# One trunk step on one core: p turned ahead by VectorE and kept in memory, the embedding weight in four transfers, and another order at the end

## The chip, the cores and the metric

The kernel runs on one core of a Trainium2 chip. Time is device time of one execution, in microseconds (us). The engines of a core are TensorE (PE in the profile; PEld is its loading of weights), VectorE (DVE), ScalarE (ACT), GpSimd (POOL) and SyncE (SP), each with its own queue of instructions in an order fixed when the program is built. Transfers are issued by SP, POOL or ACT, wait in that engine's queue like any other instruction, and run on 16 shared DMA engines.

## The reference

One layer over 2048 prompt rows and 32 sample rows of width 1024. All is float32.

```
hn   = rmsnorm(h, g_mix)
proj = hn @ w_in                      # 1024 -> 3072: hA bA cA zA vB zB
y    = concat(conv mixer, pooling mixer)
h    = h + y @ w_out                  # 1024 -> 1024
gate = sigmoid(rmsnorm(h, g_ple) @ w_ple_gate)
h    = h + (p @ w_ple) * gate         # p: 256 wide, w_ple: 256 -> 1024
return rmsnorm(h, g_final), states of the two mixers
```

The part that the change is about is `p @ w_ple`, called the embedding here, and the gate's last rows.

## The kernel before

Rows are taken in 17 tiles: 16 of 128 prompt rows and one of 32 sample rows. A float32 product is made of three: each operand is cut into a high and a low part (`split`, L76: ScalarE copies the high part, L77, VectorE subtracts it from the operand, L80), and hi x hi, hi x lo and lo x hi are added up in PSUM. The large products also use seven sub-products in the place of eight (`seven`, L212): two tiles of rows and the halves of the inner and outer dimension make 2 x 2 blocks, sums of blocks are formed by VectorE, and the results are put together from the banks x, y and z.

The stages, in the order of time:

- the input projection in three groups of columns of the turned rows (L580): groups 0 and 1 by seven products, group 2 plainly. Beside a group's products, work for later ones (turning of x, sums of its blocks) is fed in small steps: `at_pace(steps, num, den)` (L1163) takes `num` steps in `den` calls, one call being made at a fixed place in the product. In group 1 this work is `last_block` (L1149), which makes ready the rows of group 2 and stores them by POOL to memory (`b_d`).
- the early embedding: tiles 0 to 2 (`early_embedding`, L1116), begun beside the last products of group 2
- the output product with `w_out` (banks x_o, y_o, z_o, L169), beside which the gate weight is scaled (tiles `gs`, loaded by POOL, stored to `g_d`)
- the rest of the embedding: tiles 3 to 14 and the sample tile as `rest_e`, thirteen in all; the last two of them are run after the first rows for the gate have been turned
- the gate product (x_g, y_g, z_g), pair by pair; with each pair the addition to h, the final norm and the store
- the last pair, tiles 14 and 15 (`last_pair`), with the embedding of tile 15 (bank `e_l`) in it.

`embed` (L106) does the embedding of a list of tiles. `prep` loads four tiles' p at a time by SP (L123, tile `ep`), turns a tile of 128 x 256 by two transposes on TensorE into a PSUM bank (L132, tile `ptp`), and splits it from there into `pps`. `run` keeps two tiles ahead of itself, multiplies (L104, twice six products of 128 x 128 with 512 columns) and ScalarE and SP take the result to memory (`e_d`, L149 and L150). The embedding's weight `w_ple` has two tiles of 128 rows, each loaded by one transfer, at three places (`wp`, `wq`, `wl`).

The gate weight is read back from `g_d` into buffers `xh` (three of them) as `wg_r`, eight loads by SP, and split and summed by VectorE and ScalarE. The rows for the gate are turned on TensorE (`turned`, tile `pth`, L1399) for the upper tile of a pair and the sample tile, and by VectorE (`turned_here`, L1410) for the lower one: a stream transpose turns every 32 x 32 block of a tile, and the load puts the blocks at their places. All these loads are issued by SP.

In the last pair (`finish`, L1488 to L1509; `out`, L1518) each half of a tile runs through the sigmoid (ScalarE), multiplication with the embedding and addition to h (VectorE), a square summed over the row (ScalarE, `junk`), and a multiplication with the final norm's weight (`hg`). When both halves are there, POOL makes the row's factor (L1500 to L1503), VectorE and ScalarE scale half a row each, and the two halves are stored. `between` (argument 5 of `seven`) puts the embedding of tile 15's second half into the middle of the last products; its first half comes after the last.

A planner with estimates of costs sets the order of instructions on each engine, from the program's order, buffers and the estimates; an instruction given to `tc.keep_in_program_order` stays in the program's order.

## Time and profile before

| | |
|---|---|
| median of 3 executions | 929.99 us (929.95 to 930.98) |
| the profiled execution, its own time | 931.64 us |
| its span, first to last instruction | 929.9 us |
| TensorE busy | 914.6 us, 4581 products |
| VectorE, ScalarE, POOL busy | 717.1, 483.4, 127.5 us |
| bytes moved | 190.05 MB, mean 204 GB/s |

Times in the profile are microseconds from the start of the span; "L104" is line 104 of the kernel. In a row of the timeline or the chain the first number is the start, the second the duration. "x12" is a count of instructions taken together. The chain of waits is followed back from the last instruction: at each step to what released it, or to the instruction before it on its engine. A row "engine tile L <- releaser" in the list of waits has total us, times and the longest.

### The profile page before, as it was taken

How to read it: one execution, taken by the hardware profiler on the slowest of the kernel's cores; microseconds unless marked ns; L12 is line 12 of the kernel's file. 1: busy time of each engine (PE TensorE's matmuls, PEld its weight loads, DVE VectorE, ACT ScalarE, POOL GpSimd, SP SyncE). 2: the span in 40 equal slices, each digit the busy share in tenths (PEclk: the TensorE clock that was granted, in tenths of full speed). 3: DMA queues.
4: the chain of work that ended last, by engine and by line, in shares of the span. 5: the costliest groups of instructions: out<-in, count | busy, mean ns of one | idle time of the engine just before them, and what ended most of it. 6: DMA issues, size and time to landing. Idle time of an engine off the chain costs nothing.

```text
span 929.9 us, 13092 instructions
## 1 busy us (share of the span) xinstructions
PE 914.6 (98%) x4581; PEld 827.7 (89%) x4581; DVE 717.1 (77%) x1215; ACT 483.4 (52%) x895; POOL 127.5 (14%) x244
## 2 busy tenths in 40 slices
PE   7999999999999999999999999999999999999996
PEld 6999999999999999999999987888878868888885
DVE  6996989999577778585777679656564797888985
ACT  7744565654445544443545356344344865555664
POOL 3111222121001110000000011112111001111113
PEclk9999999999999999999999999999999999999999
DMA  8357687798935457337665359876775883666563
GB/s 245 100 148 217 173 255 223 222 306 298 408 100 179 136 175 215 96 102 263 200 178 168 127 207 286 241 201 202 222 219 187 309 263 119 215 223 239 184 209 114
DMA packets 133791, 190.05 MB, mean 204 GB/s; under 512 B 11740, under 2 KB 101084, under 8 KB 132445
## 3 DMA queue, kind: packets, MB, share of 16 engines
q1 hardware_dynamic: 117741, 138.78, 47.7%
q0 software_dynamic: 13248, 44.93, 14.9%
q10 hardware_dynamic: 2736, 5.51, 1.9%
q8 instruction: 36, 0.59, 0.3%
q14 instruction: 30, 0.25, 0.1%
HBM read 129.59 MB, written 59.58 MB: 203 GB/s over the span
## 4 chain that ended last, share of the span: by engine, by line
PE 89%; DVE 4%; DMA 3%; ACT 2%; issue 1%; POOL 0%; SPq 0%; POOLq 0%; ACTq 0%; DVEq 0%
PE x_o L169 9%; PE x_g L169 9%; PE x_ch L580 6%; PE x_zab L580 6%; PE x_zbv L580 6%; PE z_g L169 5%; PE z_o L169 4%; PE e L104 4%; PE z_ch L580 3%; PE z_zab L580 3%; PE h L580 3%; PE z_zbv L580 3%; PE b L580 3%; PE za L580 3%; PE zb L580 2%; PE c L580 2%
## 5 line engine op out<-in xcount | busy, mean ns | idle before, releaser
L77 ACT CAST y_S<-y_fS 128x512 fp32r<-128x512 f32 x32 | 19.5, 622 | 42.7 <-PE x_o L169 20.4
L104 PE MATMUL e<-wq,pps 128*128 128x512 f32 (+1 forms) x156 | 38.9, 400 | 0.2 <-ACT pps L77 0.2
L169 PE MATMUL x_g<-wg_b,g_S 128*128 128x512 f32 x128 | 35.9, 390 | 0.0
L169 PE MATMUL x_o<-wo_b,y_S 128*128 128x512 f32 x128 | 35.6, 390 | 0.0
L580 PE MATMUL x_zbv<-B,w_zbv_S 128*128 128x416 f32 x168 | 34.3, 352 | 0.0
L580 PE MATMUL z_ch<-B,w_ch_S 128*128 128x416 f32 x168 | 34.2, 352 | 0.0
L580 PE MATMUL z_zbv<-B,w_zbv_S 128*128 128x416 f32 x168 | 34.1, 351 | 0.0
L580 PE MATMUL z_zab<-B,w_zab_S 128*128 128x416 f32 x168 | 34.1, 351 | 0.0
L580 PE MATMUL x_zab<-B,w_zab_S 128*128 128x416 f32 x168 | 34.1, 351 | 0.0
L580 PE MATMUL x_ch<-B,w_ch_S 128*128 128x416 f32 x168 | 34.0, 351 | 0.0
L104 PEld LDWEIGHTS e<-wq,pps 128*128 128x128 f32 (+1 forms) x156 | 27.4, 182 | 7.0 <-ACT pps L77 0.5
L580 PEld LDWEIGHTS x_ch<-B,w_ch_S 128*128 128x128 f32 x168 | 31.4, 188 | 0.3
L580 PEld LDWEIGHTS z_zbv<-B,w_zbv_S 128*128 128x128 f32 x168 | 31.3, 188 | 0.3
L580 PEld LDWEIGHTS x_zab<-B,w_zab_S 128*128 128x128 f32 x168 | 31.4, 188 | 0.3
L580 PEld LDWEIGHTS z_zab<-B,w_zab_S 128*128 128x128 f32 x168 | 31.3, 188 | 0.3
L580 PEld LDWEIGHTS z_ch<-B,w_ch_S 128*128 128x128 f32 x168 | 31.3, 188 | 0.4
L580 PEld LDWEIGHTS x_zbv<-B,w_zbv_S 128*128 128x128 f32 x168 | 31.2, 188 | 0.4
L69 POOL TENSOR_SCALAR ms_f<-ssq_f 128x1 f32<-128x1 f32 (+1 forms) x15 | 8.8, 586 | 161.4 <-ACT junk L90 161.4
L77 ACT CAST y<-y 128x512 fp32r<-128x512 f32 x24 | 14.9, 619 | 28.7 <-PE x_o L169 14.1
L1237 DVE TENSOR_TENSOR c_o<-x_o,x 128x512 f32<-128x512 f32 x14 | 9.7, 692 | 25.3 <-PE x_o L169 25.3
L414 DVE SCALAR_TENSOR_TENSOR xt<-xt,rstd_x,g_bc 128x1024 f32<-128x1024 f32 (+2 forms) x14 | 17.9, 1282 | 14.5 <-POOL rstd_x L73 13.4
L1438 DVE SCALAR_TENSOR_TENSOR h<-h,rstd_f,g_bc 128x1024 f32<-128x1024 f32 (+1 forms) x15 | 19.3, 1285 | 12.7 <-POOL rstd_f L73 12.7
(583 smaller groups left out, 2677.6 us busy)
## 6 DMA issues: line engine op xcount, KB each, us to landing
y<-y_d SPq DMA_DIRECT2D x16, 512.0 KB, 9.5
x<-in_x_prompt_dram SPq DMA_DIRECT2D x16, 512.0 KB, 6.0
h_d<-x SPq DMA_DIRECT2D x16, 512.0 KB, 4.2
h<-h_d SPq DMA_DIRECT2D x16, 512.0 KB, 3.9
xt<-in_x_prompt_dram SPq DMA_DIRECT2D x15, 512.0 KB, 7.1
e<-e_d SPq DMA_DIRECT2D x15, 512.0 KB, 5.3
out_dram<-h POOLq DMA_DIRECT2D x14, 512.0 KB, 3.0
p_dT<-T POOLq DMA_DIRECT2D x12, 512.0 KB, 5.9
```

Source lines behind the costliest of these rows:

```text
L69: nc.gpsimd.tensor_scalar(ms[:n], ssq[:n], scalar1=1.0 / D, scalar2=EPS, op0=ALU.mult, op1=ALU.add)
L77: ins = nc.scalar.copy(hi, src)
L104: nc.tensor.matmul(ps[:n], pps[:, a, k, :n], wp[k][b][:, cs], start=k + q == 0, stop=k == 1 and q == 2)
L169: nc.tensor.matmul(ps[:n], lhs[:, k, a, :n], w[b][:, k], start=start and k + q == 0, stop=k == KH - 1 and q == 2, skip_group_check=True)
L414: nc.vector.scalar_tensor_tensor(xt[:n], xt[:n], r[:n], g_bc[:n], op0=ALU.mult, op1=ALU.mult)
L580: nc.tensor.matmul(ps[:, :NB], lhs[:, k, x], b[:, k, y], start=start and k + q == 0, stop=stop and k == KH - 1 and q == 2, skip_group_chec ...
L1237: add = lambda o, a, b: nc.vector.tensor_tensor(o, a, b, op=ALU.add)
L1438: nc.vector.scalar_tensor_tensor(h[:n], h[:n], rf[:n], g_bc[:n], op0=ALU.mult, op1=ALU.mult)
```

## The change

p is turned once, early: the new `turn_p`, beside group 1 behind `last_block`, loads four tiles of p by POOL so that a stream transpose of VectorE completes the turn, splits it and stores high and low parts by POOL into a new tile `pp_d` in memory (256 KB for a tile of 128 rows). The steps of group 1 are taken at 1/2 in the place of 1/3. `embed` no longer turns anything; it loads `pps` from `pp_d`, up to four tiles ahead: early tiles by SP, the rest by POOL, the last tile by SP. As the stream transpose leaves the inner index of p in another order, the rows of `w_ple` are loaded in that order too, as four transfers of 32 rows (`load_ple`).

The gate weight's raw tiles take buffers of `ya` and `xh` in turn in the place of `xh` alone; the rows for the gate of the sample tile and of the first pair are loaded by POOL in the place of SP; the sample tile's parts are kept in one buffer of `ya` in the place of two in `cmb`.

In the last pair, tile 15's embedding is made in two banks of 256 columns for its last half; multiplication and addition go part by part in program order; the square of tile 15's other half stands behind the last sigmoid (`norm`, called later); the multiplication by the norm's weight of that half is VectorE's; and a row is scaled in 640 columns by VectorE and 384 by ScalarE in the place of 512 each.

```diff
     g_d = tc.dram_tile([D, D], F32, name="g_d")
+    pp_d = tc.dram_tile([NT, P, 2 * PLE], F32, name="pp_d")
...
-    def embed(todo, wp, ring, queue=nc.sync):
+    def load_ple(t, k):
+        for q in range(4):
+            r = (2 * q + k) * 32
+            nc.sync.dma_start(t[q * 32:q * 32 + 32], w_ple[r:r + 32])
+    def load_pps(t, i, queue):
+        n = tiles[i][1]
+        queue.dma_start(t.rearrange("p a k n -> p (a k) n")[:, :, :n].bitcast(F32),
+                        pp_d[i].rearrange("p (a n) -> p a n", a=4)[:, :, :n])
+        return t
+    def embed(todo, wp, ring, queue=nc.sync, loads=nc.sync):
...
         def prep(c):
-            if c in got or c >= len(todo):
-                return
...
-            ptp = tbank(f"ptp_{i}")
-            for k in range(2):
-                nc.tensor.transpose(ptp[:, k * P:k * P + n], pt[:n, k * P:(k + 1) * P], ident[:n, :n])
-            v = ptp.rearrange("p (k t) -> p k t", k=4)[:, :2, :n]
-            split(pps[:, 0, :, :n], pps[:, 1, :, :n], v)
-            got[c] = pps
+            if c not in got and c < len(todo):
+                got[c] = load_pps(ring("pps", todo[c]), todo[c], loads)
...
             r, n = tiles[i]
-            prep(c)
-            prep(c + 1)
-            prep(c + 2)
+            for ahead in range(4):
+                prep(c + ahead)
...
-    def load_rows(pool, name, i, pr, sa=None):
+    def load_rows(pool, name, i, pr, sa=None, queue=nc.sync):
...
         t = ring4(pool, f"{name}_{i}")
-        nc.sync.dma_start(t[:n], pr[r:r + n] if sa is None else rows_of(pr, sa, r, n))
+        queue.dma_start(t[:n], pr[r:r + n] if sa is None else rows_of(pr, sa, r, n))
...
                 raw = ring4(raws, f"raw_{name}{k}")
-                nc.sync.dma_start(raw, w_ple[k * P:(k + 1) * P])
+                load_ple(raw, k)
...
                     to_memory(b_d[:, half * KH:half * KH + KH], f"b_4_{c}_{half}", pt, c * P, x[1])
+                    yield
+        def turn_p():
+            def load(a):
+                t = ring4(xin, f"p_{a}")
+                for q in range(4):
+                    part, cs = t[q * 32:q * 32 + 32], slice(q * 64, q * 64 + 64)
+                    if a < NT - 1:
+                        nc.gpsimd.dma_start(part.rearrange("p (m c) -> p m c", c=64),
+                                            p_p[a * P:(a + 4) * P, cs].rearrange("(m p) c -> p m c", p=32))
+                    else:
+                        nc.gpsimd.dma_start(part[:, :64], p_s[:, cs])
+                return t
+            rounds = [*range(0, NT - 1, 4), NT - 1]
+            t = load(0)
+            yield
+            for a, after in zip(rounds, rounds[1:] + [None]):
+                w = D if a < NT - 1 else 64
+                nc.vector.transpose(t[:, :w], t[:, :w])
+                v = t[:, :w]
+                if after is not None:
+                    t = load(after)
+                yield
+                for b in range(0, 4 if w == D else 1, 2):
+                    s = staged(f"pps_{a + b}").rearrange("p a h n -> p (a h n)")
+                    for c in range(2 if w == D else 1):
+                        i = a + b + c
+                        n = tiles[i][1]
+                        o = s[:, c * 2 * PLE:(c + 1) * 2 * PLE].rearrange("p (a k n) -> p a k n", a=2, k=2)[:, :, :, :n]
+                        if n == P:
+                            src = v[:, (b + c) * PLE:(b + c + 1) * PLE].rearrange("p (g k r) -> p k g r", g=4, k=2)
+                            hi, lo = (o[:, h].rearrange("p k (g r) -> p k g r", g=4) for h in range(2))
+                        else:
+                            src = v.rearrange("p (k r) -> p k r", k=2)
+                            hi, lo = o[:, 0], o[:, 1]
+                        split(hi, lo, src)
+                        nc.gpsimd.dma_start(pp_d[i].rearrange("p (a n) -> p a n", a=4)[:, :, :n],
+                                            o.rearrange("p a k n -> p (a k) n").bitcast(F32))
...
                     if j == 1:
-                        aside = at_pace(last_block(), 1, 3)
+                        aside = at_pace(chain(last_block(), turn_p()), 1, 2)
...
-        def short(name, parts, n):
+        def short(name, parts, n, pool=None):
             A = []
+            if pool is not None:
+                both = pool.tile([P, 2, KH, P], F32R, tag="t", name=f"{name}_a")
             for half, t in enumerate(parts):
-                c = cmb.tile([P, KH, 2, P], F32R, tag="c", name=f"{name}_{half}")
-                c = c.rearrange("p k h n -> p k (h n)")
+                c = (cmb.tile([P, KH, 2, P], F32R, tag="c", name=f"{name}_{half}").rearrange("p k h n -> p k (h n)")
+                     if pool is None else both[:, half])
...
                 raw = ring4(ya, f"{name}r_{k}")
-                nc.sync.dma_start(raw, w_ple[k * P:(k + 1) * P])
+                load_ple(raw, k)
...
-        _, run = embed(rest_e, wp, ring)
+        _, run = embed(rest_e, wp, ring, loads=nc.gpsimd)
...
         for k in range(KH):
-            raw = [ring4(xh, f"wg_r{k}_{i}") for i in range(2)]
+            raw = [ring4(t, f"wg_r{k}_{i}") for i, t in enumerate(((ya, ya), (ya, xh), (xh, xh), (ya, ya))[k])]
...
+        hn_queue = [nc.gpsimd]
...
             r, n = tiles[i]
-            t = load_rows(ya, "hn", i, h_d).rearrange("p (q k c) -> p k q c", q=4, k=KC)
+            t = load_rows(ya, "hn", i, h_d, queue=hn_queue[0]).rearrange("p (q k c) -> p k q c", q=4, k=KC)
...
             for q in range(4):
-                nc.sync.dma_start(t[q * 32:q * 32 + 32].rearrange("p (g c) -> p g c", g=4),
+                hn_queue[0].dma_start(t[q * 32:q * 32 + 32].rearrange("p (g c) -> p g c", g=4),
...
-            pt = ring4(ya, "p_l")[:, :PLE]
-            nc.sync.dma_start(pt, p_p[(i + 1) * P:(i + 2) * P])
+            pps = load_pps(ss.tile([P, 2, 2, P], F32R, tag="s", name="pps_l"), i + 1, nc.sync)
...
-            def embedded():
...
-            def finish(b, half, ee, m):
+            def finish(b, half, parts):
...
                 t = gate[b, half]
-                parts = [(slice(o, o + m), slice(half * NH + o, half * NH + o + m)) for o in range(0, NH, m)]
-                for cs, fs in parts:
-                    tt(t[:, cs], ee[:, cs], t[:, cs], op=ALU.mult)
-                    tt(h[b][:, fs], h[b][:, fs], t[:, cs], op=ALU.add)
-                    ssq = sm.tile([P, 1], F32, tag="ssq", name=f"ssq_l{b}{half}_{cs.start}")
-                    nc.scalar.activation(junk[:, fs], h[b][:, fs], AF.Square, scale=D ** -0.5, accum_out=ssq)
+                where = []
+                for cs, ee in parts:
+                    fs = slice(half * NH + cs.start, half * NH + cs.stop)
+                    where.append(fs)
+                    for o, x, op in (t[:, cs], ee, ALU.mult), (h[b][:, fs], h[b][:, fs], ALU.add):
+                        ins = tt(o, x, t[:, cs], op=op)
+                        if len(parts) > 1:
+                            tc.keep_in_program_order(ins)
+                return lambda: norm(b, half, where)
+            def norm(b, half, where):
+                for fs in where:
+                    ssq = sm.tile([P, 1], F32, tag="ssq", name=f"ssq_l{b}_{fs.start}")
+                    ins = nc.scalar.activation(junk[:, fs], h[b][:, fs], AF.Square, scale=D ** -0.5, accum_out=ssq)
+                    if b:
+                        tc.keep_in_program_order(ins)
...
                 second = half != b
-                for _, fs in parts:
-                    (nc.vector if second else nc.gpsimd).tensor_tensor(hg[b][:, fs], h[b][:, fs], g_bc[:, fs], op=ALU.mult)
+                for fs in (where if b == 0 else [*where, slice(half * NH + NH, half * NH + 2 * NH)] if second else []):
+                    ins = (nc.vector if second else nc.gpsimd).tensor_tensor(hg[b][:, fs], h[b][:, fs], g_bc[:, fs], op=ALU.mult)
+                    if b:
+                        tc.keep_in_program_order(ins)
...
                     return
-                if len(parts) > 1:
+                if len(where) > 1:
...
                 o, y = hg[b], y_p[r:r + P]
-                nc.vector.tensor_scalar(o[:, :NH], o[:, :NH], scalar1=rf, scalar2=None, op0=ALU.mult)
-                nc.sync.dma_start(y[:, :NH], o[:, :NH])
-                nc.scalar.activation(o[:, NH:], o[:, NH:], AF.Copy, scale=rf)
-                (nc.scalar if b else nc.gpsimd).dma_start(y[:, NH:], o[:, NH:])
+                cut = 5 * P
+                nc.vector.tensor_scalar(o[:, :cut], o[:, :cut], scalar1=rf, scalar2=None, op0=ALU.mult)
+                nc.sync.dma_start(y[:, :cut], o[:, :cut])
+                nc.scalar.activation(o[:, cut:], o[:, cut:], AF.Copy, scale=rf)
+                (nc.scalar if b else nc.gpsimd).dma_start(y[:, cut:], o[:, cut:])
...
                 if b == 0:
-                    finish(b, half, e[:, half * NH:half * NH + NH], NH)
+                    finish(b, half, [(slice(0, NH), e[:, half * NH:half * NH + NH])])()
...
             def second(half, m):
-                ps = bank(f"e_l{half}")
-                embed_product(ps, pps, wp, slice(half * NH, half * NH + NH))
-                finish(1, half, ps, m)
-            pps = embedded()
-            seven(f"g{i}", A, W, carry, out, {5: lambda: second(1, NH)}, first_tile=True)
-            second(0, NH // 2)
+                parts = []
+                for o in range(0, NH, m):
+                    ps = bank(f"e_l{half}_{o}")
+                    embed_product(ps[:, :m], pps, wp, slice(half * NH + o, half * NH + o + m))
+                    parts.append((slice(o, o + m), ps[:, :m]))
+                return finish(1, half, parts)
+            later = []
+            seven(f"g{i}", A, W, carry, out, {5: lambda: later.append(second(1, NH))}, first_tile=True)
+            later[0]()
+            second(0, NH // 2)()
...
         n = tiles[NT - 1][1]
-        A = short("gl", turned(NT - 1), n)
+        A = short("gl", turned(NT - 1), n, ya)
...
             step()
+        hn_queue[0] = nc.sync
```

20 lines of the change are left out of this document (removed).

## The prediction

> **What bounds the kernel now.** I read the page first: busy time by engine, then the shares of the chain that ended last.
>
> ```profile
> PE 914.6 (98%) x4581; PEld 827.7 (89%) x4581; DVE 717.1 (77%) x1215; ACT 483.4 (52%) x895; POOL 127.5 (14%) x244
> PE 89%; DVE 4%; DMA 3%; ACT 2%; issue 1%; POOL 0%; SPq 0%; POOLq 0%; ACTq 0%; DVEq 0%
> ```
>
> TensorE is busy 914.6 of 929.9 us, so work taken from its queue shortens the run, unless something else becomes late. Next I read the chain of waits in the rest of the embedding stage and behind it, then the transposes of p as a tile.
>
> ```profile
> 708.44 2.72 PE x_o L169 x12
> 711.17 0.23 PE ptp L132 x2
> ...
> 711.42 0.38 ACT pps L77
> ...
> 715.09 0.22 PE ptp L132 x2
> 715.31 2.77 PE e L104 x12
> 718.07 0.22 PE ptp L132 x2
> ...
> 743.08 5.80 DMA wg_r<-g_d
> ...
> 766.14 1.88 PE x_g L169 x7
> ```
>
> ```profile
> L132 PE MATMUL ptp<-ident,ep x32: 222/272/328, 536.2 to 742.0; 128*128 128x128 f32 x30, 32*128 32x32 f32 x2
> ...
> L80 DVE TENSOR_TENSOR pps<-ptp,pps x16: 220/419/426, 537.4 to 743.0; 128x256 fp32r<-128x256 f32 x15, 128x64 fp32r<-128x64 f32 x1
> L1479 PE MATMUL ptp_l<-ident,p_l x2: 270/270/271, 897.0 to 897.2; 128*128 128x128 f32 x2
> ```
>
> Each tile of the rest of the embedding is two transposes (0.22 us) and twelve products (2.77 us). The period is 718.07 - 715.09 = 2.98 us. Twelve products of the same shape without a transpose between them take 2.72 us (708.44). From 743.08 on the chain runs through a transfer of the gate weight and then VectorE, until the gate product at 766.14.
>
> **The change part by part.**
>
> *Transposes of p leave TensorE.* Rest of the embedding, 13 tiles: 13 x (2.98 - 2.72) = 3.4 us, and the first tile's transpose and copy before any product, 711.17 to 711.80, 0.4 us more than the 0.26 counted for it: 3.8. Counted over the whole stage it is a little more:
>
> ```profile
> 745.07 0.68 PE L1399 MATMUL pth<-ident,ho 32*128 32x32 f32 x8
> ...
> 751.32 0.85 PE L272 MATMUL x_gl<-wg_c,gl 128*64 128x512 f32 x3
> ```
>
> The next product starts at 751.32, 40.15 us after 711.17. What must stay is 156 products by 0.227 us (2.72 / 12), 35.4, and some 0.6 of the transposes pth. That leaves 4.15; I take 4.2 us, since it holds the restarts too. Early embedding, three tiles:
>
> ```profile
> 536.34 0.22 PE ptp L132 x2
> ...
> 537.13 0.28 PE ptp L132 x2
> ...
> 541.39 0.22 PE ptp L132 x2
> ```
>
> 0.22 + 0.28 + 0.22 = 0.72 us. Last pair: the two ptp_l overlap, 0.27 us by the row of 270 ns. Together 5.2 us on TensorE, all on the path, because its queue has no idle time there beside the first wait.
>
> *The same p turned by VectorE in group 1.* Four stream transposes of 128x1024, a small one, seventeen copies on ScalarE and as many subtractions on VectorE, fed at one step in two instead of one in three.
>
> ```profile
> L1410 DVE STREAM_TRANSPOSE hn<-hn x8: 1237/1239/1241, 752.7 to 891.7; 128x1024 f32<-128x1024 f32 x8
> ```
>
> ```profile
> core 0: us, PE busy (x) PEld busy (x) DVE busy (x) ACT busy (x) POOL busy (x), PEclk, DMA share, GB/s
> 325.00:350.00 25.00, 25.00 (x138) 24.10 (x137) 18.62 (x32) 12.12 (x25) 4.38 (x6) 1.00 0.53 165
> 350.00:375.00 25.00, 25.00 (x135) 24.44 (x134) 19.58 (x31) 11.57 (x21) 1.00 (x2) 1.00 0.69 206
> 375.00:400.00 25.00, 25.00 (x135) 24.74 (x134) 15.77 (x27) 10.51 (x19) 0.00 (x0) 1.00 0.34 103
> 230.00:255.00 25.00, 25.00 (x134) 24.74 (x133) 13.78 (x24) 9.77 (x18) 0.54 (x1) 1.00 1.02 411
> 711.00:751.00 40.00, 39.76 (x190) 30.95 (x189) 29.13 (x53) 32.46 (x69) 1.07 (x3) 1.00 0.83 293
> ```
>
> VectorE gets 4 x 1.24 + 17 x 0.42 = 12.1 us, ScalarE 17 x 0.38 = 6.5 us. In the built order this work stands between about 345 and 400 us, where VectorE has 1.3 + 5.4 + 9.2 = 15.9 us idle (a fifth of the first row, and all of the next two) and ScalarE over 27. The work is hidden by TensorE's own 100%, but leaves VectorE 3.8 us of slack in 55. If that cover fails, what is late are the weight splits that VectorE makes for the next product. Bounds: 0 us, or, if all 12.1 fell on one block of twelve that waits, 12.1; I take 0.3, as the idle time exceeds the work. Two transposes of x that group 1's order moves into the middle of a product could also stall it, by less than one copy, 0.38 us; it lies inside the 0.3.
>
> *Queues.* The stores of the turned p, 17 of 256 KB, go out by POOL, where POOL is busy 0 to 1 us in 25 (350 to 400). Its load for group 2 stands behind them, and waits for TensorE anyway, by the list of waits:
>
> ```profile
> POOL hn L1183 <- PE y_zab L580: 62.1, 1, 62.1
> ```
>
> The 17 issues would have to take 3.6 us each to fill that. SP's first loads of y and of the output weight, 2.5 MB, move from about 360 to 400 us and wait for the last of these stores; they are wanted after 540 us, so that costs 0. The p of group 1 itself comes by POOL in 128 KB pieces; the nearest row is the turned rows by SP:
>
> ```profile
> hn<-h_d SPq DMA_DIRECT2D x33, 128.0 KB, 3.0
> ```
>
> Even several times that only moves the work later, to y's loads 140 us ahead of their use: 0. The 16 loads of 256 KB replace loads of p of half the size. In the rest of the embedding 13 of them go by POOL, into four slots, and the loads of the turned rows for the gate now stand among them.
>
> *The weight of the embedding by four transfers.* Six more issues by SP at three places, where the weight is not the last thing awaited. Such an issue took this long:
>
> ```profile
> 897.46 0.33 SPq L1356 DMA_DIRECT2D wlr<-in_w_ple_dram  x1
> ```
>
> I take 0, since TensorE is busy beside them; at most the six issues of one place, 2 us. At best the four parts land sooner than one transfer, which nobody waits for: 0 too.
>
> *Buffers of the gate weight, rows for the gate by POOL.* Five of the eight loads of the gate weight can be issued before the embedding stage, so the chain through 743.08 moves ahead. It buys nothing by itself, as TensorE is busy there; it is needed for the 4.2 us to last beyond 766 us. VectorE also loses 13 x 0.42 = 5.5 us of subtractions in that stage. I take 0 lost, at most the whole 4.2.
>
> *The new loads by POOL.* The nearest rows, from the page, and, for the first of them, from the answer on its own line, are these:
>
> ```profile
> gs<-in_w_ple_gate_dram POOLq DMA_DIRECT2D x16, 256.0 KB, 9.2
> ...
> wg_r<-g_d SPq DMA_DIRECT2D x8, 512.0 KB, 5.2
> ```
>
> ```profile
> DMA to landing us min/median/max: 6.4/9.2/11.4
> ```
>
> The same queue and size took 9.2 us in the output stage; loads of twice the size in and around the embedding stage itself, by SP, 5.2. A load is issued when the tile four before it is done, and wanted three tiles later, 3 x 2.72 = 8.2 us. I take it as in time, at no cost, by the rows of the same stage; the other end is the first rival.
>
> The Trainium skill, "DMA: Bandwidth & Descriptors", section on the anatomy of one DMA, fits 2.0 us plus bytes over 436 GB/s to a load issued by GpSimd, an estimate of 2.6 us for 256 KB, by which nothing would be lost here. The row of 9.2 us disagrees with it. The same page, section "SWDGE vs HWDGE vs iDMA", speaks against the change: GpSimd writes its descriptors into memory that VectorE locks it out of in one of its modes, while transfers by SP are immune. By that rule the loads could be late as in the first rival; no run so far shows which of the two holds here.
>
> *The end.*
>
> ```profile
> 917.80 2.89 PE L169 MATMUL x_g<-wg_T,g 128*128 128x512 f32 x12
> 920.53 1.52 PE L104 MATMUL e_l<-wl,pps_l 128*128 128x512 f32 x6
> 921.20 0.63 ACT L1491 ACTIVATE junk<-h 128x512 bf16<-128x512 f32 x1 [0.44 <-DVE h L1489]
> 921.83 0.67 ACT L1518 ACTIVATE g_l<-x_g,rs_h 128x512 f32<-128x512 f32 x1
> 922.53 0.76 DVE L1488 TENSOR_TENSOR g_l<-e_l,g_l 128x256 f32<-128x256 f32 x2 [1.41 <-ACT g_l L1518]
> 923.20 0.75 DVE L1489 TENSOR_TENSOR h<-h,g_l 128x256 f32<-128x256 f32 x2
> 923.65 0.42 ACT L1491 ACTIVATE junk<-h 128x256 bf16<-128x256 f32 x1 [1.15 <-DVE h L1489]
> ...
> 925.02 0.57 POOL L1503 TENSOR_TENSOR rstd_l<-ssq_l,nhalf 128x1 f32<-128x1 f32 x1
> 925.62 0.72 ACT L1508 ACTIVATE hg<-hg,rstd_l 128x512 f32<-128x512 f32 x1 [1.06 <-POOL rstd_l L1503]
> ```
>
> The sigmoid of the last half starts at 921.83 although its product ended at 920.69 (917.80 + 2.89): ScalarE does the square of the other half first. In front of that square it starts near 920.75, a gain of 1.08 us. The embedding product must then be ready: six products of 512 end at 922.05, of which a first part of 256 columns is ready halfway, 921.3, before the sigmoid's 921.44. Multiplication, addition and square now wait for one another in parts; the displaced square (0.63) fills the gap before the first small square. I take 0.95 us gain, between 0 (ScalarE's order is given back in the squares) and 1.2 (the smaller last scaling too: 384 columns instead of 512 of 0.72 us, 0.18 less).
>
> The sum: 0.7 + 4.2 + 0.3 + 0.95 = 6.15 us, less 0.3, is 5.85. The profiled execution took 931.64 us (span 929.9 and 1.7 around it); it would be 925.8. It stands 1.65 above the median of 929.99, which so becomes 924.1.
>
> **The rivals.**
>
> *Loads by POOL come late (slower side).* One mechanism: four slots, each refilled when its tile ends. With landing time L a tile takes (L + 2.72) / 4 where that is over 2.72. Four tiles are loaded ahead and nine can wait. At the 9.2 us of the gate weight the period is 2.98, and 924.1 + 9 x 0.26 = 926.4. At the longest of them, 11.4 us, it is 3.53: 924.1 + 9 x 0.81 = 931.4. It is slower by more than 0.2% (931.85) from L = 11.6 on, which a little more traffic than in the output stage would bring; at 12.4 (11.4 and 1 us behind the gate's loads on the same queue) it is 3.78 a tile and 933.6. For it: the transfers. 293 GB/s over 40 us are 11.7 MB; 13 loads bring 1.7 MB more, the earlier gate weight takes some 1.5 away, and the rest in 36 us is 330 GB/s, where the share was 0.83. Against it: the row of 411 GB/s at 230 us.
>
> *The chain into the gate.* VectorE's work from 743.08 to 766.14 stays where it is, for the transfer or the rows come no earlier; TensorE waits up to 4.2 us before the gate product. Only 0.7 + 0.3 + 0.95 - 0.3 = 1.65 us are left: 928.3. For it: VectorE is the chain there now. Against it: the earlier loads and 5.5 us less work.
>
> *Group 1 stalls.* VectorE's 3.8 us of slack is not enough at one block, 1 to 3 us: 925 to 927. For it: VectorE would be busy 93% of 55 us. Against it: the shares of before left no product waiting there (25.00 of 25.00).
>
> *The end gives nothing.* 924.1 + 0.95 = 925.05.
>
> **How the numbers follow.** The forecast, with its own range of 922.3 (all bounds at their best) to 925.7 (some 1.6 of small stalls), 0.50. The end gives nothing, 0.05, inside that range. Group 1 stalls, 0.12. Loads by POOL late by about the 9.2 us, 0.10. These are faster, 0.77 together: what a measurement of this kernel can tell from no change is about 0.2%, 1.9 us, so faster ends at 928.1. The chain into the gate, or loads between 10 and 11.6 us, no change within 1.9 us: 0.09. Loads at 11.6 us or more, slower: 0.14. The range of 922.2 to 930.0 leaves out some 0.14 above and 0.04 below.
>
> **What would show it.** Right: no ptp on TensorE; products of e every 2.72 us from about 705 us (shifted by 0.7) with no idle time; x_g behind it 5 us earlier than 766.14; TensorE 100% between 345 and 400; sigmoid of g_l at once behind the last x_g, and the last scaling near 924.7 less the earlier 5.3. Wrong: PE or its weight load waiting for a load of pps; its landing over 8 us; the gate product waiting for VectorE; idle time of TensorE in group 1.

## The result and the profile after

The changed kernel takes 927.75 us (median of 8 executions, 926.63 to 929.13) against 930.81 us (8 executions) for the kernel before on the same chip. The ratio is 0.9968, with a 95% interval of 0.9959 to 0.9977: 0.32%, or 3.1 us, faster. One execution of the kernel before took 1135 us and is left out of the ratio. The forecast was 5.85 us. Two later comparisons of the unchanged pair gave 0.9973 both times. The profiled execution took 929.13 us, span 927.2.

The page of the changed kernel first: busy time by engine, and the group of the embedding's products.

```profile
PE 912.1 (98%) x4553; PEld 826.3 (89%) x4553; DVE 719.7 (78%) x1221; ACT 483.5 (52%) x895; POOL 159.6 (17%) x299
L105 PE MATMUL e<-wq,pps 128*128 128x512 f32 (+1 forms) x156 | 36.2, 391 | 0.9 <-DMA pps<-pp_d 0.9
```

TensorE has lost 34 transposes of p and gained six products at the end (two banks of 256 columns in the place of one), 28 instructions and 2.5 us of busy time less. The last column of the second row says that TensorE stood still before these products for 0.9 us, for a load of the kept p. The timeline of TensorE in the stage shows where; a row has start, duration and, in brackets, idle time and releaser.

```profile
711.68 13.76 PE L105 MATMUL e<-wq,pps 128*128 128x512 f32 x60
726.30 16.61 PE L105 MATMUL e<-wq,pps 128*128 128x512 f32 x72 [0.86 <-DMA pps<-pp_d]
742.84 0.68 PE L1435 MATMUL pth<-ident,ho 32*128 32x32 f32 x8
743.45 5.80 PE L105 MATMUL e<-wq,pps 128*128 128x512 f32 x24
749.08 1.08 PE L264 MATMUL x_gl<-wg_c,gl_a 128*64 128x512 f32 x4
```

The first row of the same stage in the kernel before, from the same view:

```profile
711.01 0.60 PE L132 MATMUL ptp<-ident,ep 128*128 128x128 f32 x4
```

No `ptp` stands between the products any more. The stage lasts 749.08 - 711.68 = 37.40 us, against 751.32 - 711.01 = 40.31 before: 2.91 us less, where 4.15 was worked out. (The prediction's 40.15 begins at the chain's mark of 711.17, where the product ahead has ended; the timeline, in which neighbours overlap, has 711.01.) After five tiles (60 products) the sixth waits. The chain of waits at that place (start, duration, what), POOL's issue of the loads for the fifth and the sixth tile (from POOL's timeline), and the landing times of the loads in the stage:

```profile
719.03 7.14 DMA pps<-pp_d
726.17 0.14 issue
726.30 16.61 PE e L105 x72
```

```profile
715.35 0.61 POOL L115 DMA_DIRECT2D pps<-pp_d  x1
719.03 0.54 POOL L115 DMA_DIRECT2D pps<-pp_d  x1 [3.07 <-PE e L105]
```

```profile
DMA to landing us min/median/max: 3.5/5.8/7.6
```

In group 1 the extra work of VectorE fits, as the windows (length, busy time and count of each engine, clock, DMA share, GB/s) show: TensorE is at 25.00 of 25.00 while VectorE is at 24.00. But earlier in the group, at 304 us, TensorE waits for a tile of x to be turned; the timeline has it.

```profile
350.00:375.00 25.00, 25.00 (x135) 24.75 (x134) 24.00 (x41) 13.46 (x26) 9.62 (x16) 1.00 0.86 234
375.00:400.00 25.00, 25.00 (x134) 24.75 (x133) 19.68 (x38) 12.79 (x28) 6.35 (x12) 1.00 0.58 171
```

```profile
303.79 1.28 DVE L406 SCALAR_TENSOR_TENSOR xt<-xt,rstd_x,g_bc 128x1024 f32<-128x1024 f32 x1 [0.73 <-POOL rstd_x L74]
305.22 0.95 PE L413 MATMUL pt<-ident,xt 128*128 128x128 f32 x7 [0.68 <-DVE xt L406]
```

The last pair and the end, by the chain (first two rows) and by the timelines of ScalarE, VectorE and POOL:

```profile
908.98 0.48 ACT c_g L1455
...
909.50 3.03 PE z_g L161 x12
```

```profile
908.25 0.63 ACT L1529 ACTIVATE junk<-h 128x512 bf16<-128x512 f32 x1 [1.18 <-DVE h L1521]
```

```profile
918.48 0.69 ACT L1561 ACTIVATE g_l<-x_g,rs_h 128x512 f32<-128x512 f32 x1
...
920.52 0.42 DVE L1521 TENSOR_TENSOR h<-h,g_l 128x256 f32<-128x256 f32 x1
920.86 1.38 DVE L1535 TENSOR_TENSOR hg<-h,g_bc 128x256 f32<-128x256 f32 x3
...
921.63 0.66 POOL L1543 TENSOR_TENSOR ssq_l<-ssq_l,ssq_l 128x1 f32<-128x1 f32 x1 [0.60 <-ACT junk L1529]
922.37 0.57 POOL L1545 TENSOR_TENSOR rstd_l<-ssq_l,nhalf 128x1 f32<-128x1 f32 x1
922.97 0.61 ACT L1551 ACTIVATE hg<-hg,rstd_l 128x384 f32<-128x384 f32 x1 [1.48 <-POOL rstd_l L1545]
```

The sigmoid starts 0.03 us after the last x_g (915.72 + 2.73 by the chain). The last scaling starts at 922.97; POOL's addition of one column took 0.66 us. In the kernel before, ScalarE's order around the same copy of c_g was the other one, copy first and square (`junk`) behind it:

```profile
911.09 0.59 ACT L1419 COPY c_g<-z_g 128x512 f32<-128x512 f32 x1 [1.12 <-PE z_g L169]
...
913.57 0.63 ACT L1491 ACTIVATE junk<-h 128x512 bf16<-128x512 f32 x1 [1.89 <-DVE h L1489]
```

Laid side by side by the starts of the first products of each stage in the timeline of TensorE, one execution of each kernel differs as follows (what lies ahead of 300 us is left out):

| stretch | before | after | gain | forecast |
|---|---|---|---|---|
| group 1, `x_ch` at 300 us to the `z_ch` behind the last transposes of x | 53.98 | 54.91 | -0.93 | -0.3 |
| last `za` of group 2 to first x_o (early embedding) | 18.34 | 17.62 | 0.72 | 0.7 |
| output product, first x_o to the rest of the embedding | 161.13 | 161.46 | -0.33 | 0 |
| rest of the embedding | 40.31 | 37.40 | 2.91 | 4.2 |
| first x_g to e_l (all pairs) | 156.72 | 156.86 | -0.14 | 0.3 |
| e_l to the end | 13.43 | 13.01 | 0.42 | 0.95 |
| sum | | | 2.65 | 5.85 |

The spans differ by 2.7 us (929.9 and 927.2), so the table holds nearly all of it. The output product has no term of the change; it took between 161.1 and 162.1 us in the traced executions of all the kernels here, so its 0.33 us is no sign of a cost. Each of the other terms except the early embedding fell short. The experiments ask why, and whether the shortfalls can be won back.

### The profile page after: what moved, and what is told of

Its sections match the earlier page's. It is cut to its first block, busy times and chain, and to the rows that moved or that the text cites. A ratio compares the mean times of both kernels' runs of the same rounds, so it can differ in the third digit from the quotient of the medians.

```text
span 927.2 us, 13211 instructions
## 1 busy us (share of the span) xinstructions
PE 912.1 (98%) x4553; PEld 826.3 (89%) x4553; DVE 719.7 (78%) x1221; ACT 483.5 (52%) x895; POOL 159.6 (17%) x299
## 4 chain that ended last, share of the span: by engine, by line
PE 60%; DVE 2%; DMA 2%; issue 1%; ACT 1%; POOL 0%; POOLq 0%; SPq 0%; DVEq 0%; ACTq 0%
PE x_g L161 8%; PE x_o L161 8%; PE z_g L161 4%; PE z_o L161 4%; PE e L105 3%; PE x_zab L572 3%; PE x_ch L572 2%; PE y_g L161 2%; PE x_zbv L572 2%; PE b L572 2%; PE v L572 2%; PE c L572 2%; PE zb L572 2%; PE h L572 2%; PE za L572 2%; PE y_o L161 2%
## 5 line engine op out<-in xcount | busy, mean ns | idle before, releaser
L105 PE MATMUL e<-wq,pps 128*128 128x512 f32 (+1 forms) x156 | 36.2, 391 | 0.9 <-DMA pps<-pp_d 0.9
L161 PEld LDWEIGHTS x_o<-wo_b,y_S 128*128 128x128 f32 x128 | 23.9, 188 | 5.6 <-ACT y_S L78 0.4
```

The costliest lines, as they stand in the source:

```text
L105: nc.tensor.matmul(ps[:n], pps[:, a, k, :n], wp[k][b][:, cs], start=k + q == 0, stop=k == 1 and q == 2)
L161: nc.tensor.matmul(ps[:n], lhs[:, k, a, :n], w[b][:, k], start=start and k + q == 0, stop=k == KH - 1 and q == 2, skip_group_check=True)
```

## The experiments

All edits are made to the changed kernel. Ratios are to the kernel before, run on the same chip.

**The pair again.** No edit.

> The changed kernel as it is, for a second trace. Theory: the 0.68 us that TensorE waits for xt in group 1 and the wait for a load of pps in the embedding stage (0.86 us) are there again, as both come from the order of the queues; the time is 926.5 to 929.1, 0.2 to 0.45% below the kernel before. Rival: the wait for pps is chance of that one execution; then it is absent here or at another tile, and the span is about 1 us shorter than 927.2.

928.57 us, ratio 0.9973 (0.9963 to 0.9983). The waits are at the same places: 0.68 us at 304, 0.52 at the sixth tile, 0.37 before z_g at 909. The stage of the embedding takes 37.01 us. The waits belong to the kernel, not to one execution; of these three only the sixth tile's size varies.

**The loads of the kept p by SP.**

```diff
-        _, run = embed(rest_e, wp, ring, loads=nc.gpsimd)
+        _, run = embed(rest_e, wp, ring)
```

> The loads of pps in the rest of the embedding by SP in the place of POOL. Theory of late loads: what was lost in the stage (2.75 us gained of 4.2) is lost by the issue and landing on POOL's queue; then no wait for pps is left and the time is 0.8 to 1.4 us below the changed kernel. Rival (the transfers as a whole are dense there, 365 GB/s, whichever queue issues them): loads land after 5 us or more here too, a wait of about the same size stays, and the time is that of the changed kernel within 0.5 us, or worse, as SP's queue has them between the stores of e that wait for ScalarE.

935.58 us, 1.0055 (1.0039 to 1.0070): slower than before. TensorE's timeline shows two waits, and the landing times in the stage (705 to 760 us) follow.

```profile
729.39 16.80 PE L105 MATMUL e<-wq,pps 128*128 128x512 f32 x73 [1.42 <-DMA pps<-pp_d]
760.38 0.73 PE L161 MATMUL x_g<-wg_c,g 128*128 128x512 f32 x2 [2.48 <-ACT g L78]
```

```profile
DMA to landing us min/median/max: 7.2/7.7/8.2
```

The profile has the landing of only two of these loads, issued at 723.40 and 725.99: 8.2 and 7.2 us. POOL's loads of the same moments in the changed kernel (720 to 726 us) took 6.8 to 7.6 us. So by SP they land no sooner, and the stage takes 38.54 us. The larger loss is behind it: at the first x_g TensorE waits 2.48 us for the gate's rows. The loads stand on SP's queue among the gate's loads and the stores of e; how much of the loss each of these makes was not tried. In the prediction the Trainium skill, "DMA: Bandwidth & Descriptors", section "SWDGE vs HWDGE vs iDMA", spoke for SP: transfers by SP are immune to VectorE's lock. These rows neither show that lock nor refute it; if it cost POOL's loads something here, it was less than the move to SP cost.

**Six slots for the kept p, six tiles ahead.**

```diff
-            for ahead in range(4):
+            for ahead in range(6 if loads is nc.gpsimd else 4):
...
-                return st.tile([P, 2, 2, P], F32R, tag="t", name=f"pps_{i}")
+                c = rest_e.index(i)
+                own = (ss, "s") if c % 6 in (1, 4) else (st, "t")
+                return own[0].tile([P, 2, 2, P], F32R, tag=own[1], name=f"pps_{i}")
```

> Six slots in the place of four for the turned p in the rest of the embedding (two of the three buffers ss beside the four of st), and loads up to six tiles ahead. Theory: the wait of 0.5 to 0.86 us at the sixth tile comes from a slot that is refilled too late; with six slots it is gone, and from the first product of the stage to x_gl pass 36.4 to 36.6 us in the place of 37.0 to 37.4. The time falls by 0.5 to 0.9. Rival: the loads are late because the 16 DMA engines are full there; then the same wait comes at another tile and the stage keeps its 37 us.

927.38 us, 0.9973 (0.9964 to 0.9982). The stage is now what the prediction said of the products; TensorE's timeline, at the start of group 2 and in the stage:

```profile
433.01 2.53 PE L572 MATMUL zb<-hn,w_zb 128*128 128x416 f32 x12 [0.38 <-DMA hn<-b_d]
```

```profile
712.62 30.08 PE L105 MATMUL e<-wq,pps 128*128 128x512 f32 x132
...
748.89 1.08 PE L264 MATMUL x_gl<-wg_c,gl_a 128*64 128x512 f32 x4
```

Eleven tiles run without a break, and the stage takes 748.89 - 712.62 = 36.27 us. So the refill of a slot was the missing 1.1 us. Yet by the times the kernel is no faster than the changed one: this execution lost about 1 us at the start of group 2 (first row), a place the edit does not touch. It need not be a price of the six slots: the unedited kernel lost 0.8 us at the same place in its third trace (`after_3` below, with a wait of 0.22 us for hn), and nothing in its first two.

**The gate weight in `xh` alone, as before.**

```diff
-            raw = [ring4(t, f"wg_r{k}_{i}") for i, t in enumerate(((ya, ya), (ya, xh), (xh, xh), (ya, ya))[k])]
+            raw = [ring4(xh, f"wg_r{k}_{i}") for i in range(2)]
```

> The raw gate weight in three buffers xh alone, as before the change. The rival chain into the gate of the prediction: without the earlier loads TensorE waits 2 to 4 us in front of x_g, and the gain of the embedding stage is gone (930 to 931 us). If the loads were not what held the chain, TensorE waits less than 0.5 us there and the time is that of the changed kernel.

936.95 us, 1.0082 (1.0070 to 1.0095). TensorE waits at the door of the gate product, as the second rival described, and longer than the 2 to 4 us expected:

```profile
753.70 1.97 PE L264 MATMUL x_gl<-wg_c,gl_a 128*64 128x512 f32 x4 [5.83 <-DVE gl_a L81]
```

The buffers in `ya` win nothing by themselves, and without them the whole gain and more is lost.

**The end as before.** The last pair's `finish`, `out` and `second` of the kernel before, with everything else changed.

```diff
-            def finish(b, half, parts):
+            def finish(b, half, ee, m):
...
-                cut = 5 * P
-                nc.vector.tensor_scalar(o[:, :cut], o[:, :cut], scalar1=rf, scalar2=None, op0=ALU.mult)
+                nc.vector.tensor_scalar(o[:, :NH], o[:, :NH], scalar1=rf, scalar2=None, op0=ALU.mult)
```

> The changed kernel with the end of the kernel before (the embedding of tile 15 in banks of 512 columns, the square in front of the last sigmoid, halves of 512 columns in the scaling). By the two traces the new end is worth 0.49 us from the start of the last x_g: this kernel is 0.4 to 0.6 us slower than the changed one. By the prediction it would be 0.95. Rival: the new end gives nothing, 0.

928.48 us, 0.9977 (0.9968 to 0.9987): by the times no different from the changed kernel. In the traces, from e_l to the end, it takes 13.32 us against 13.01. The new end is worth 0.3 to 0.4 us.

**VectorE's product of h and the norm's weight, made short.** Over 384 columns only; for the other 640 it is done in the one operation that scales.

```diff
-                for fs in (where if b == 0 else [*where, slice(half * NH + NH, half * NH + 2 * NH)] if second else []):
+                cut = 5 * P
+                for fs in (where if b == 0 else [slice(cut, D)] if second else []):
...
-                nc.vector.tensor_scalar(o[:, :cut], o[:, :cut], scalar1=rf, scalar2=None, op0=ALU.mult)
+                if b:
+                    nc.vector.scalar_tensor_tensor(o[:, :cut], h[b][:, :cut], rf, g_bc[:, :cut], op0=ALU.mult, op1=ALU.mult)
+                else:
+                    nc.vector.tensor_scalar(o[:, :cut], o[:, :cut], scalar1=rf, scalar2=None, op0=ALU.mult)
```

> At the end VectorE multiplies only 384 columns of tile 15 by the norm's weight before the factor is there, and does the other 640 with the scaling in one operation. Theory: POOL's sum in front of the factor took 0.66 us instead of 0.19 because VectorE was multiplying beside it; with VectorE idle it takes 0.19, the last scaling starts 0.4 us earlier, its operation is 0.25 longer, and the span from the last x_g is 0.15 to 0.25 us shorter (11.64 to about 11.45). Rival: POOL's sum takes 0.5 us or more also with VectorE idle.

928.03 us, 0.9983 (0.9973 to 0.9993), which says nothing of so small a term. The trace does: e_l to the end takes 12.62 us instead of 13.01. The timelines of VectorE and POOL:

```profile
920.49 0.58 DVE L1536 TENSOR_TENSOR hg<-h,g_bc 128x384 f32<-128x384 f32 x1
922.13 0.88 DVE L1550 SCALAR_TENSOR_TENSOR hg<-h,rstd_l,g_bc 128x640 f32<-128x640 f32 x1 [1.07 <-POOL rstd_l L1546]
```

```profile
921.26 0.19 POOL L1544 TENSOR_TENSOR ssq_l<-ssq_l,ssq_l 128x1 f32<-128x1 f32 x1 [0.60 <-ACT junk L1529]
```

With VectorE done at 921.07, POOL's addition takes 0.19 us; in the changed kernel, beside VectorE's product, it took 0.66 and ended at 922.29, when that product ended too (922.24). The Trainium skill, "GPSIMD Engine Reference", section "Specifications", says that GpSimd shares its interfaces to SBUF with VectorE, with contention from instructions of VectorE with two inputs in SBUF, as this product has. The two rows agree, and give it a price here: 0.47 us on an operation of one column, which lasted as long as what was left of the product.

**The old pace for `last_block`.** 1/3 as before for the first 37 calls, in which `last_block` gets through its twelve steps, then 1/2 for `turn_p`.

```diff
-                        aside = at_pace(chain(last_block(), turn_p()), 1, 2)
+                        aside = two_paces(last_block(), (1, 3), turn_p(), (1, 2))
```

> The steps of group 1 at 1/3 until the rows of group 2 are done, as before, then at 1/2 for turning p. Theory: the faster pace moved the transposes of x into the middle of a product; with the old pace the wait of 0.68 us is gone and group 1 loses 0 to 0.3 us against the kernel before in the place of 0.93: 0.6 to 0.9 us below the changed kernel. Rival: VectorE, busier for a shorter time behind it, makes the weights late instead, and TensorE waits 0.5 us or more between 350 and 425 us: no gain or a loss.

934.85 us, 1.0046 (1.0031 to 1.0062). The wait at 304 is gone, but two others stand in group 2, by the list of waits:

```profile
PE pm L825 <- ACT pp L78: 2.9, 1, 2.9
PE zb L572 <- DMA hn<-b_d: 2.5, 1, 2.5
```

The last store into `pp_d` landed only at 424.95, and group 2's rows `hn` after it.

**A middle pace.** 2/5 for `last_block`, 3/5 for `turn_p`.

```diff
-                        aside = at_pace(chain(last_block(), turn_p()), 1, 2)
+                        aside = two_paces(last_block(), (2, 5), turn_p(), (3, 5))
```

> The steps of group 1 at 2/5 until the rows of group 2 are done, then at 3/5: turning p ends as in the changed kernel, and the transposes of x stand between whole products again. Theory: the 0.68 us of waiting at 304 us are gone, and group 1 loses 0.2 us or less against the kernel before in the place of 0.93; no wait of 2.45 us before group 2, because the last store of p is no later. Time 0.6 to 0.9 us below the changed kernel. Rival: VectorE, with the same work in fewer calls, is late with weights between 340 and 400 us, 0.3 us or more of waits of TensorE there.

934.93 us, 1.0049 (1.0037 to 1.0061). Group 1 takes 53.90 us, as before the change (53.98), so the pace of `last_block` was the cause of the 0.93 us. But the time is lost again in group 2. The timelines of TensorE and SP's queue:

```profile
434.15 2.54 PE L572 MATMUL zb<-hn,w_zb 128*128 128x416 f32 x12 [2.11 <-DMA hn<-b_d]
453.15 0.57 PE L825 MATMUL pm<-pp,pw 128*128 128x416 f32 x1 [2.85 <-ACT pp L78]
```

```profile
414.17 0.37 SPq L308 DMA_DIRECT2D y<-y_d  x1
...
416.85 2.05 SPq L313 DMA_DIRECT2D wo_q<-in_w_out_dram  x4
...
419.55 10.68 SPq L509 DMA_DIRECT2D raw_h<-in_w_in_dram  x1
430.32 3.75 SPq L509 DMA_DIRECT2D raw_za<-in_w_in_dram  x1
```

SP's first loads of y, x and wo_q, which wait for the last store of p, go out at 414 to 419 us and meet the two loads of hn (419). SP then stands 10.68 us at one issue, and the raw weights behind it are late. This made a new theory: the 2.5 MB that the prediction moved at a cost of 0 are what the repairs run into.

**The same, with these loads behind group 2's first weights of wo** (some 439 us); and two combinations: `late_two` has pace 1/2, six slots and the short product, `best` the pace 2/5 beside them.

```diff
...
-                first_y = load_y(0, 2 * P)
-                first_x = load_rows(ya, "x", 0, x_p)
...
+                if gi == 2 and j == 0:
+                    ya = ctx.enter_context(tc.tile_pool(name="ya", bufs=5, side="right"))
+                    first_y = load_y(0, 2 * P, wo_load)
+                    with tc.issue_after(wo_load.ins):
+                        first_x = load_rows(ya, "x", 0, x_p)
...
```

> The kernel pace25 (last_block at 2 of 5 steps, turn_p at 3 of 5) with one move: SP's first loads of the output product (y, x and the four of wo_q, 2.5 MB) stand behind the load of wo_r for the first unit of group 2, some 436 us, instead of 408 to 419 us. Theory: in pace25 these loads collided with the two hn<-b_d loads (issued at 419, landed at 429.45 and 434.11) and held SP's raw loads, and that made the waits of 2.11 us at 432 and 2.85 us at 450. With the loads away from there both waits go (under 0.5 us together), the wait of 0.68 us at 304 stays away, and the kernel runs 0.5 to 1.0 us below the changed kernel's 928.3: 927.3 to 927.8. Rival: the waits come from the later stores into pp_d themselves (VectorE and GpSimd still busy with p at the group's start): then 2.0 us or more of waits stay between 425 and 455 us and the time is 932 or more. Second rival: the loads, now at 436 us, come too late for group 2's raw weights or for the output product: then a wait shows between 440 and 500 us or before the first frame sums of the output product.

> The changed kernel, its pace of 1 of 2 kept, with three edits: the same later place for SP's first y, x and wo_q loads; six slots for the loads of pps in the rest of the embedding (two of them from the pool of the short sums), taken six tiles ahead; and VectorE's product of hidden row and weight at the end over 384 columns instead of 1024, the other 640 in the one operation that scales. Theory: the terms add: about 0.5 to 0.9 us for the sixth tile's wait (36.3 us for the stage), 0.3 to 0.4 us at the end, and group 2 no longer pays the 1.0 us that six slots alone lost at 432 us, since hn<-b_d no longer shares the DMA with the y loads: 926.9 to 927.5, that is 0.9 to 1.4 us below the changed kernel. The wait of 0.68 us at 304 stays. Rival (the six slots' loss at group 2 has another cause than the y loads): a wait of 0.3 us or more stays at 432 us and the kernel is within 0.5 us of the changed one.

> All of it: late_two with the paces of late_y (2 of 5, then 3 of 5). Theory: late_two's gain and the 0.7 to 0.9 us of group 1: 925.9 to 926.7, 1.6 to 2.4 us below the changed kernel and 4.0 to 5.0 us below the kernel before, with the sum of the prediction's terms (5.85 us) reached to within the 0.4 us wait of the last pair and the small waits left in the rest of the embedding. Rival: waits at 425 to 455 us as in pace25: 931 or more.

`late_y`: 931.60 us, 1.0009 (1.0000 to 1.0019). `late_two`: 930.33, 0.9991 (0.9979 to 1.0003). `best`: 931.21, 1.0004 (0.9993 to 1.0014). All three are misses. In `late_y` the wait for hn is gone and the ratio is 0.0040 (3.7 us) below that of the pace alone, but one of 2.56 us has come at 453. TensorE's timeline and the windows of `late_two`, which has the same one:

```profile
457.06 0.40 PE L1079 MATMUL pst<-ident,st 128*34 128x128 f32 x1 [2.63 <-DVE st L1071]
```

```profile
453.00:456.00 3.00, 1.43 (x8) 1.08 (x6) 2.89 (x8) 2.25 (x5) 0.00 (x0) 1.00 1.20 290
456.00:459.00 3.00, 1.94 (x7) 1.86 (x8) 2.96 (x12) 1.42 (x4) 0.90 (x2) 0.65 1.00 262
459.00:462.00 3.00, 3.00 (x14) 2.93 (x13) 0.94 (x4) 0.62 (x1) 1.12 (x3) 0.78 0.67 185
462.00:465.00 3.00, 3.00 (x18) 2.97 (x17) 1.76 (x3) 0.62 (x1) 0.00 (x0) 1.00 0.48 167
```

The loads, now at 439 to 443 us, stand right ahead of the raw weights of the next unit (raw_zb, raw_v at 443 to 445), which land late: raw_v takes 9.4 us, against 5.0 in the changed kernel. The column before the DMA share is the granted clock: behind the wait it is 0.65 and 0.78 for 6 us, so that the wait costs more than its 2.63 us. Whether the place of the loads is the whole cause was still open.

**The loads in a quiet place**: behind the raw weight b of group 2's third unit (some 486 us), where the next raw weight is issued 13 us later.

```diff
+            raw_load[kind] = nc.sync.dma_start(t, w_in[:, col:col + P].rearrange("(k p) n -> p k n", p=P))
...
+                    wo_load = raw_load["b"]
+                if gi == 2 and j == 2:
...
```

> late_y with SP's 2.5 MB of first y, x and wo_q loads in a third place: behind the load of raw_b of group 2's third unit (some 486 us), where the next raw weights are issued 13 us later. Theory: the loads move the wait to whatever raw load stands behind them (hn<-b_d in pace25, raw_v of the second unit in late_y); behind raw_b none is near, so no wait over 0.4 us between 425 and 540 us, and no lower granted clock there. late_y lost 2.56 us in the wait at 453 and about 1.7 us more in the 6 us behind it, where the clock was 0.65 to 0.8; with both gone: 931.6 less 3.9 to 4.3, that is 927.3 to 927.7 against a kernel before of 931.0. Rival: the waits belong to group 2's start itself: one of 2 us or more stays between 425 and 460 us, 930 or more.

> late_two (pace 1 of 2 kept, six slots for the last embedding tiles, the shorter VectorE product at the end) with the loads in the place of quiet_y. Theory: the wait of 2.63 us at 454 and the 1.7 us behind it go: 926.0 to 926.6 on this scale (before at 931.0), with the wait of 0.68 us at 304 still there. Rival: a new wait before the first frame sums of the output product (542 to 550 us), if the loads are late for it: 927 or more.

> quiet_two with the paces 2 of 5 and 3 of 5 of quiet_y. Theory: the wait at 304 goes too (0.7 to 0.9 us): 925.1 to 925.9, 5.1 to 5.9 us below the kernel before, which is the prediction's sum of 5.85 us less the last pair's 0.4 us. Rival: hn<-b_d stays late with these paces even without the loads of y (best waited 0.70 us at 430.5): then 0.3 to 0.7 us of it remain and the kernel is no faster than quiet_two.

`quiet_y` (with the pace of 2/5): 929.67 us, 0.9974 (0.9963 to 0.9985). The wait of 2.56 us and the lower clock are gone, but 1.11 us for hn is left at 432. `quiet_two` (pace 1/2, six slots, short product): 926.91 us, **0.9944 (0.9931 to 0.9956)**. `quiet_best` (both): 928.72 us, 0.9959 (0.9946 to 0.9971). The theory of the place holds: from `pace25` to `quiet_y` only the place of 2.5 MB differs, and the ratio falls by 0.0075. It holds for the combination too: from `late_two` to `quiet_two` again only the place differs, and the ratio falls by 0.0047 (by 0.0034 with the second run of `quiet_two` below). TensorE's timeline in `quiet_two` has no break in eleven tiles; in `quiet_best` the rival came true:

```profile
710.60 30.08 PE L105 MATMUL e<-wq,pps 128*128 128x512 f32 x132
...
746.86 1.08 PE L264 MATMUL x_gl<-wg_c,gl_a 128*64 128x512 f32 x4
```

```profile
432.67 2.53 PE L574 MATMUL zb<-hn,w_zb 128*128 128x416 f32 x12 [1.27 <-DMA hn<-b_d]
```

With the pace that frees group 1, TensorE comes to group 2 0.6 us earlier and waits 1.3 us for the 3.3 MB of hn, which land 1.5 us later than in `quiet_two` (432.63 against 431.16). The cause of that lateness is not settled; the last store of p lands at 413.25 there, against 406.72.

**The parts of that gain, on one chip.** The changed kernel; it with the quiet place alone; and `quiet_two` again.

> The changed kernel again, on the chip of the two that follow, so that they can be compared with it: 3 us below the kernel before (0.9965 to 0.9975).

> The changed kernel with one edit: SP's first y, x and wo_q loads behind raw_b of group 2's third unit instead of at 408 us. Theory: in the changed kernel these loads cost nothing, as the prediction has it (no wait at 425 to 455 us in its trace); they only use up the slack that other edits would need. So it is within 0.4 us of the changed kernel. Rival: they cost something that the trace of one execution does not show: 0.5 us or more below it.

> quiet_two again: six slots, the short VectorE product and the later place together, 1.4 to 2.6 us below the changed kernel on the same chip (six slots 1.1, the end 0.4, the rest the execution's own spread) and 4.6 to 5.4 us below the kernel before.

`after_3`: 928.17 us, 0.9973 (0.9961 to 0.9985). `quiet_after`: 928.85, 0.9974 (0.9965 to 0.9984). `quiet_two_3`: 926.90, **0.9957 (0.9945 to 0.9969)**. The place alone wins nothing, as expected. The three edits together are 0.0016 below the changed kernel here, 1.5 us, as much as the stage (37.40 - 36.25 = 1.15) and the end (13.01 - 12.62 = 0.39) give in the traces; the intervals of these two still overlap, while that of the first run of `quiet_two` (up to 0.9956) lay below that of the changed kernel (from 0.9959). By its median it is the fastest of the kernels shown, both times. The rest of the larger gain in that first run is not from the edits, as far as its trace tells: of the 2.6 us between the spans of `quiet_two` and the first trace of the changed kernel, 1.5 are in the stage and at the end; 0.8 are ahead of 300 us, where nothing was edited, and 0.35 in the output product, whose time differs by 1.0 us between the two traces of `quiet_two` itself. `quiet_after` waits 1.76 us at the sixth tile (1.8 in the list of waits), which shows how far this wait can go with four slots:

```profile
PE e L105 <- DMA pps<-pp_d: 1.8, 1, 1.8
```

## Why the prediction was right or wrong

The direction was right, and so was the reason: work taken from a TensorE that is busy 98% shortens the run. The size was not: 3.1 us instead of 5.85, outside the forecast's own range (922.3 to 925.7 on a scale where before is 929.99; the result is 927.0 there, 0.9968 of it). By its steps:

- **Early embedding, 0.7.** Right: 0.72 us by the trace.
- **Rest of the embedding, 4.2.** The step that failed is "I take it as in time, at no cost" of the loads by POOL. The work on TensorE was right: with six slots the stage takes 36.25 to 36.27 us in six executions, 4.05 less than before by the same marks. With four slots it took 37.40, 37.01 and 37.04 in the unedited kernel. The step gave a load 8.2 us, from the end of the tile that frees its slot. The first refill, for the fifth tile, was issued at 715.35 and was in time (wanted at 722.56). The second was late: the sixth tile's slot came free when the second tile ended, near 717.1 us, but its load was issued at 719.03, 1.9 us later, and needed 7.14 us to land. So 6.4 us were left for 7.14. The landing time by itself stayed inside the 8.2; what the step left out is the delay of the issue. The rival of late loads had the right mechanism and the wrong form: it is one wait at the second refill, 0.2 to 1.8 us by execution, and not a longer period of every tile. The 2.6 us that the fit of the Trainium skill, "DMA: Bandwidth & Descriptors", section on the anatomy of one DMA, gave for such a load were not met in this stage: its loads took 3.5 to 7.6 us, 5.8 in the median. POOL's row names a product of e as what this load waited for; by the times it is one half-way through the third tile. Why it had to wait for that one, and not for the last of the second tile, the runs do not show. The next two were issued 0.4 us behind their tiles.
- **Group 1, less 0.3.** A term mis-sized: 0.93 us. The prediction had named the two transposes of x moved into the middle of a product and bounded their stall by one copy, 0.38 us. What TensorE waits for there is not a copy, but VectorE's scaling of the tile, 1.28 us from 303.79, behind POOL's row factor; it cost 0.68 us. The pace decides it (`two_paces`, `pace25`). VectorE's own load was judged rightly: 24.00 of 25.00 us and no wait of TensorE there.
- **The last pair, 0.3.** The transposes are gone, but TensorE waits 0.38 us before z_g at 909 for ScalarE's copy of c_g. That wait is in every kernel of the changed form and not in the list of before. It is something that becomes late next, which the sum did not look for. The rows above show what ScalarE did instead: it took the square of tile 14's half at 908.25 ahead of the copy at 908.88, where the kernel before had the copy first and the square 2.5 us behind it. `old_end` has the same wait, so the new end is not its cause; another order on ScalarE was not tried.
- **The end, 0.95.** A term mis-sized: 0.42 us. The sigmoid came first as worked out, but the last addition to h came only 0.76 us earlier, measured from the start of e_l, and POOL's addition beside VectorE's product took 0.66 instead of 0.19 us. `hg_short` took that product away and won 0.39 us in the traces, more than the 0.15 to 0.25 expected of it. With it, the end gives 0.81.
- **SP's 2.5 MB of y, x and wo_q, "so that costs 0".** True of the changed kernel as far as the times tell (0.9973 for `after_3`, 0.9974 for `quiet_after`), and still a step with much behind it. The prediction asked when these loads are wanted, not what they would delay. At 408 us they leave the loads of hn (wanted at 430) just in time: no wait in two traces of the changed kernel, 0.22 us in the third. With the paces that put them at 414 or 425 us, TensorE waited twice for 2.1 to 2.9 us; behind the first weights of wo, at 437 to 443 us, once for 2.6 to 2.9 us.
- **POOL's load of hn "waits for TensorE anyway".** Right: 419.42 against 418.4.
- **The four transfers of the embedding's weight, 0.** No wait for it stands in the traces of after.
- **Buffers of the gate weight.** Right that they are needed: without them x_gl waits 5.83 us. The rival of the chain into the gate was real, and these buffers are what kept it away.

So of the 3.2 us that are missing by the table, 1.1 is the slot refill, 0.2 the rest of that stage, 0.6 the pace of group 1, 0.4 the copy before z_g, 0.4 POOL beside VectorE, 0.1 what else fell short at the end, and 0.3 the output product's own spread. The refill and POOL's part were won back in `quiet_two`. The pace's part can be won, but then comes back as a wait for hn.

## What to carry to other kernels

When TensorE is full, a saving on it is worth its whole size only if each thing that must now come sooner does: price each refill of a ring of buffers by the moment its load is really issued, and not only by the period. When a large transfer is moved, ask what stands behind it on its queue and on the DMA engines at the new place, not only when it is wanted itself; a place with no urgent load behind it was worth 3.2 to 7.0 us here between otherwise equal kernels. A small operation of POOL on the path should not run beside a VectorE operation with two inputs in SBUF; here it lasted until that one had ended.

## What the runs showed that was not expected

In these runs a wait of TensorE of some 2.5 us or more cost more than itself, since the granted clock fell behind it. Two windows each of `pace25`, behind its wait of 2.11 us (to 434.15) and its wait of 2.85 us (to 453.15):

```profile
434.20:437.00 2.80, 2.80 (x15) 2.77 (x16) 0.17 (x1) 0.83 (x2) 0.00 (x0) 1.00 1.21 290
437.00:440.00 3.00, 3.00 (x18) 2.97 (x17) 2.94 (x6) 1.90 (x4) 0.00 (x0) 1.00 1.03 247
```

```profile
453.00:456.00 3.00, 2.70 (x7) 2.23 (x8) 2.98 (x10) 2.15 (x5) 0.00 (x0) 0.56 0.96 271
456.00:459.00 3.00, 3.00 (x15) 2.95 (x15) 2.17 (x8) 0.62 (x2) 0.00 (x0) 0.88 1.11 291
```

The clock stays at 1.00 behind the first and falls to 0.56 and 0.88 behind the second, which is 3 x 0.44 + 3 x 0.12 = 1.7 us more. In all the runs waits up to 2.45 us left the clock at 1.00, and those of 2.48 (`pps_sp`), 2.56 (`late_y`), 2.63 (`late_two`), 2.85 (`pace25`), 2.87 (`two_paces`), 2.88 (`best`) and 5.83 us (`wg_xh`) lowered it to 0.50 to 0.67 for about 3 us. Each length was seen once, and 2.45 and 2.48 are so close that the length alone need not decide. The Trainium skill, "TensorE: Matmul & The Clock Gate", section on the clock gate in its part 1, has the clock fall after at least one idle window of about 3.4 us; here less was enough, and the measurement decides.

The second surprise is the spread of equal work: with four slots the stage of the sixth tile took between 37.0 and 38.3 us in kernels that differ only elsewhere (`again`, `quiet_after`), while with six slots it came out at 36.25 to 36.27 us six times. Two more slots bought steadiness beside the 1.1 us.
